# A MoE layer on one core: every chunk of an expert's weights as a high and a low part, one low part per expert on GpSimd

## The chip, the cores and the metric

The kernel runs on one NeuronCore of a Trainium2 chip. The metric is the device time of one execution in microseconds (us). The engines are named as the profile names them: PE (matrix multiplication; its weight loads are listed as PEld), DVE (vector engine), ACT (scalar engine), POOL (GpSimd) and SP (here it issues the loads of the weights). Each engine works through its own instructions strictly in order; semaphores tie the engines together.

## The reference

One layer of a decoder on 2048 tokens of width 1024: a mixer (input projection, retention heads, short convolution, output projection) and a hierarchical mixture of experts. Each token picks one of 8 groups, then 2 of that group's 8 experts, so that there are 64 experts. Everything is float32. The part that the change touches is the expert block:

```python
def run_block(args):
    tok, e = args
    xb = t_pad[tok]
    hb = jax.nn.silu(xb @ w_gate[e]) * (xb @ w_up[e])
    return hb @ w_down[e]
```

`w_gate` and `w_up` are 1024 x 512 per expert, `w_down` is 512 x 1024. The outputs of the experts are weighted, added to the residual stream, and normalised (final RMSNorm).

## The kernel before, in words

The program has two stages. The dense stage (mixer, router, lists of tokens) ends at about 940 us; then the experts run one after the other, 96 token slots each, to the end.

**One expert.** Its three matrices are cut into 24 chunks of 128 rows by 512 columns: 8 of w_gate (`w` = 0 in the code), 8 of w_up (1), and 8 of w_down (2), of which chunk `c` belongs to row block `c // 2` and column half `c % 2`. The weights arrive as units of four chunks (1 MB each, line 639, issued by SP into a set of buffers that are reused in turn).

**Split products.** A float32 product is made of three matmuls in the faster format float32r (lines 739 to 741, `mm3`): high part of the tokens times high part of the weight, high times low, low times high. The parts of a weight are made for a *piece*, which is two neighbouring chunks (128 x 1024): ACT copies the piece into float32r, which rounds it (line 679, `split_hi`), and DVE subtracts this from the original (line 685, `split_lo`). A piece has one of six places (four tiles `ring`, two tiles `part`), and its parts are made five pieces ahead (`LEAD`) of the matmuls that use it, so `split_hi` waits until PE has done with the piece that stood in that place.

**The plain chunks.** Chunks 6 and 7 of w_down (the last piece) are not split: `plain` picks them, and line 1056 multiplies them as plain float32 straight from the unit's buffer, with the third row block's tokens in `ewhole`. So an expert has 11 pieces, and DVE makes 11 low parts.

**The order of the work.** A stream written out by hand sets it: gate of expert q (8 chunks), up of q (8), then down of q-1 (8). What else an engine does is put in at places of this stream:

- PE transposes the hidden rows of q-1 after gate (line 758, `ph`), and the tokens of q+1 after up (line 730, `pxg`); ACT and DVE make their high and low parts (lines 764 and 765; 733 and 734: `xhi`, `xlo`). Before, 765 works on 128 x 288, and line 763 copies the remaining 96 columns whole.
- DVE multiplies gate and up (line 751, `hrow`), and adds the result of down to the token rows (line 778, twice per expert, from the PSUM tile `acc`).
- ACT takes the sum of squares of finished rows (line 784) and scales them (line 792).
- POOL, for each expert from the ninth on: fetches token rows by an indirect DMA (710), makes a row of weights (771), two tiny operations on the sums (785, 786), fetches residual rows (717, behind the transposes `pxg`), multiplies the rows scaled by ACT with the row of weights (795, 96 x 1024, two inputs in SBUF), and writes them out (822). For the first eight experts the rows are written without 771, 785, 786, 792 and 795.

Of the kernel before, what the change touches and what calls it, by code (L numbers as in the profile page):

```python
# [10 lines left out]
F32 = mybir.dt.float32  # L11
F32R = mybir.dt.float32r
# [3 lines left out]
AF = mybir.ActivationFunctionType  # L16
OP = mybir.AluOpType
AX = mybir.AxisListType

P = 128  # L20
# [5 lines left out]
KF = FF // P  # L26
# [5 lines left out]
CAP = 96  # L32
# [51 lines left out]
def hybrid_layer(ctx: ExitStack, tc: tile.TileContext, x, xT, norm1, w_in, gn_w, conv_w, w_o, norm2, norm2r,  # L84
                 r_w, r_b, w_gate, w_up, w_down, final_w, con, rot, empty, out):
    nc = tc.nc
    act, dve, pool, pe, sp = nc.scalar, nc.vector, nc.gpsimd, nc.tensor, nc.sync
# [47 lines left out]
    raws, parts = {}, {}  # L135
# [41 lines left out]
    hT, xraw = {}, {}  # L177
# [448 lines left out]
    EX = {}  # L626
# [18 lines left out]
    estream = []  # L645
# [15 lines left out]
            loaded.add(i)  # L661


    def plain(w, c):
        return w == 2 and c >= 6


    pieces = [(q, w, c) for q, w, c in estream if c % 2 == 0 and not plain(w, c)]
    ppos = {u: i for i, u in enumerate(pieces)}

    def split_hi(i):
# [10 lines left out]
    def split_lo(i):  # L682
        if i < len(pieces):
            hi, lo, src = parts[pieces[i]]
            dve.tensor_tensor(lo, src, hi.bitcast(F32), op=OP.subtract)  # L685

    rows_dma = {}

# [10 lines left out]
    def row_of(q):  # L699
        return row_all(q)[:CAP]  # L700
# [18 lines left out]
                                    bounds_check=S - 1, oob_is_err=False)  # L719
        moved("g", q, i)  # L720

    NH = 3

    def xpose(q):
        g, w = row_of(q), EX["work"]
        hi, lo = (w.tile([P, KD, CAP], F32R, name="x" + n) for n in ("hi", "lo"))
        for half in range(2):
            p = bank("pxg")
            for j in range(4):
                pe.transpose(p[:, j * P:j * P + CAP], g[:, half * 4 + j::KD], ident[:CAP, :CAP])  # L730
            pv = p.rearrange("p (k t) -> p k t", k=4)[:, :, :CAP]
            ks = slice(half * 4, half * 4 + 4)
            act.activation(hi[:, ks], pv, AF.Copy)
            dve.tensor_tensor(lo[:, ks], pv, hi[:, ks].bitcast(F32), op=OP.subtract)  # L734
        EX["xT", q] = hi, lo, None

    def mm3(o, ahi, alo, w, first, last):
        whi, wlo = w
        pe.matmul(o, ahi, whi, start=first, stop=False)  # L739
        pe.matmul(o, ahi, wlo, start=False, stop=False)  # L740
        pe.matmul(o, alo, whi, start=False, stop=last)  # L741
# [12 lines left out]
    def hpose(q):  # L754
        w = EX["work"]
        p = bank("ph")
        for k in range(KF):
            pe.transpose(p[:, k * P:k * P + CAP], EX["h", q][:, k::KF], ident[:CAP, :CAP])
        n = NH
        hi, lo = (w.tile([P, n, CAP], F32R, name="e" + v) for v in ("hi", "lo"))  # L760
        whole = w.tile([P, KF - n, CAP], F32, name="ewhole")
        pv = p.rearrange("p (k t) -> p k t", k=KF)[:, :, :CAP]
        act.activation(whole, pv[:, n:], AF.Copy)
        act.activation(hi, pv[:, :n], AF.Copy)
        dve.tensor_tensor(lo, pv[:, :n], hi.bitcast(F32), op=OP.subtract)
        EX["hT", q] = hi, lo, whole

    def weights(q, m=None):
        e = order[q]
# [58 lines left out]
    start = {}  # L828
# [131 lines left out]
    i = TB - 1  # L960
# [33 lines left out]
    w = ctx.enter_context(tc.tile_pool(name="work", bufs=1, side="right", reuse_waits="tile"))  # L994
# [28 lines left out]
    def later(q):  # L1023
        return q >= NG

    ps = {}
    for i, (q, wi, c) in enumerate(estream):
        if c % 4 == 0:
            done = upos[q, 2 * wi + c // 4] - 1
            if not AT <= done < AT + NFIRST:  # L1030
                load_unit(done + NRAW + (NFIRST if done < AT else 0))
        if (q, wi, c) in ppos:
            split_hi(ppos[q, wi, c] + LEAD)
            split_lo(ppos[q, wi, c] + LEAD)
        if i in (36, 40, 44):
            two = pair(FIRST[i // 4 - 9])
            if i < 44:
                EX["rows"] += two
                for j in (2, 1):
                    clear(len(EX["rows"]) - j)  # L1040
                    if i == 36:
                        gather(5 - j)
            else:
                EX["fw"], EX["fwm"] = (t[:CAP] for t in two)
                sp.dma_start(EX["fw"], bass.AP(tensor=final_w.tensor, offset=final_w.offset, ap=[[0, CAP], [1, D]]))
        n = q, 2 * wi + c // 4
        cs = slice(c % 4 * 512, c % 4 * 512 + 512)
        if plain(wi, c):
            wt = raws[n][:, cs]
        else:  # L1050
            wt = [t[:, c % 2 * 512:c % 2 * 512 + 512] for t in parts[q, wi, c - c % 2][:2]]

        def mm(o, stats, k, last):
            hi, lo, whole = stats
            if plain(wi, c):
                pe.matmul(o, whole[:, k - hi.shape[1]], wt, start=False, stop=last)  # L1056
            else:
                mm3(o, hi[:, k], lo[:, k], wt, k == 0, last)

        if wi < 2:  # L1060
            if c == 0:
                ps[wi] = acc.tile([P, 512], F32, name="acc")[:CAP]
            mm(ps[wi], EX["xT", q], c, c == 7)
            if wi == 0 and c == 0:
                if q > 1:
                    gather(q + 3)
                if later(q - 2):
                    weights(q - 2)
            if wi == 0 and c == 2 and 1 < q < NG + 2:
                put_rows(q - 2)  # L1070
            if wi == 0 and c == 4 and later(q - 2):
                norm1_rows(q - 2)
            if c == 7:
                if wi == 0:
                    gate_act(q, ps[0])
                    if q:
                        hpose(q - 1)
                else:
                    up_act(q, ps[1])
                    if q + 1 < NE:  # L1080
                        xpose(q + 1)
                        regather(q + 1)
        else:
            if c < 2:
                ps[2 + c] = acc.tile([P, 512], F32, name="acc")[:CAP]
            k, half = divmod(c, 2)
            mm(ps[2 + half], EX["hT", q], k, k == KF - 1)
            if q < NE - 1:
                if c == 4 and later(q - 1):
                    norm2_rows(q - 1)  # L1090
                    put_rows(q - 1)
                    if q == NE - 2:
                        weights(q)
                        weights(q + 1, EX["fw"])
                if c == 7:
                    add_rows(q, (ps[2], ps[3]))
                if c == 4 and q == NE - 2:
                    hpose(NE - 1)
            else:
                if c == 1:  # L1100
                    norm1_rows(q - 1)
                if c == 2:
                    r = row_of(q - 1)
                    dve.tensor_tensor(r, r, EX["m", q - 1], op=OP.mult)
                    act.activation(r, r, AF.Copy, scale=EX["ss", q - 1])
                    put_rows(q - 1)
                if c >= 6:
                    finish(q, half, ps[2 + half])
# [109 lines left out]
```

## Time and profile before

| | |
|---|---|
| median of 3 runs | 2124.74 us (2124.18 to 2127.75) |
| the profiled execution | 2125.29 us, its span 2123.5 us |
| busy over the span | PE 98%, DVE 80%, ACT 61%, POOL 38% |
| DMA | 578.81 MB, mean 273 GB/s |
| chain that ended last | lines 739 to 741 and 1056 on PE, then ACT, POOL and DVE for the last rows |

The profile lists each engine's instructions with a start and a length, and for a gap ahead of one the engine or transfer that ended it. The length of an instruction that follows another without a gap overlaps with its neighbour's a little, so what one costs is read from start to start. The length also holds the time in which an instruction stands blocked after its start. The shares are means over both stages; the expert stage is read by itself, below.

### The profile page before, as it was taken

What the parts mean: (1) busy time and instruction counts of PE and PEld (TensorE: products, weight loads), DVE (VectorE), ACT (ScalarE), POOL (GpSimd) and SP (SyncE); (2) the same over time, 40 slices, a digit from 0 to 9 for tenths busy, and PEclk for the clock granted to TensorE, in tenths of its full rate; (3) what the DMA queues carried; (4) which work ended last, traced back from release to release, by engine and by line L of the source; (5) the groups of instructions that cost most, each with busy time, mean ns of one, the idle gap of its engine ahead of it and who ended that gap; (6) DMA issues with size and microseconds to landing.
All of it is one profiled execution on the core that took longest, in us unless ns stands there. A gap on an engine that the chain in (4) does not pass through costs nothing. (4 is left out here: it accounts for less than half of the span.)

```text
span 2123.5 us, 28824 instructions
## 1 busy us (share of the span) xinstructions
PE 2087.7 (98%) x9801; PEld 1581.2 (74%) x9802; DVE 1704.2 (80%) x2460; ACT 1303.0 (61%) x1945; POOL 810.5 (38%) x871
## 2 busy tenths in 40 slices
PE   8999999999999999969999999999999999999998
PEld 7888888888888888856666666666666666666665
DVE  4657666775676467478889999999999999999997
ACT  4324433443334432458778888888888888888885
POOL 0010023001210022053334555466666666666657
PEclk9999999999999999979999999999999999999999
DMA  8345244534434354768999999999999999999991
GB/s 269 108 126 169 90 141 133 159 113 135 144 110 159 94 172 144 283 238 311 386 392 379 388 386 388 385 385 393 390 384 388 383 388 389 385 391 392 389 393 52
DMA packets 142279, 578.81 MB, mean 273 GB/s; under 512 B 29616, under 2 KB 29968, under 8 KB 92912
## 3 DMA queue, kind: packets, MB, share of 16 engines
q1 hardware_dynamic: 113456, 526.48, 66.1%
q0 software_dynamic: 28672, 50.46, 6.4%
q8 instruction: 77, 1.26, 0.2%
q14 instruction: 74, 0.61, 0.1%
HBM read 576.76 MB, written 52.59 MB: 296 GB/s over the span
## 5 line engine op out<-in xcount | busy, mean ns | idle before, releaser
L685 DVE TENSOR_TENSOR ring<-unit,ring 128x1024 fp32r<-128x1024 f32 x470 | 614.5, 1338 | 37.6 <-ACT ring L679 36.0
L679 ACT ACTIVATE ring<-unit 128x1024 fp32r<-128x1024 f32 x470 | 491.4, 1056 | 117.4 <-PE acc L741 111.5
L297 PE MATMUL acc<-hhi,ring 128*128 128x512 f32 x1280 | 404.5, 393 | 7.0 <-ACT ring L172 5.4
L685 DVE TENSOR_TENSOR part<-unit,part 128x1024 fp32r<-128x1024 f32 x234 | 309.5, 1343 | 18.2 <-ACT part L679 17.5
L173 DVE TENSOR_TENSOR ring<-wraw,ring 128x512 fp32r<-128x512 f32 x256 | 172.6, 687 | 185.3 <-ACT ring L172 185.3
L172 ACT ACTIVATE ring<-wraw 128x512 fp32r<-128x512 f32 x256 | 153.7, 625 | 264.3 <-issue 111.1
L739 PE MATMUL acc<-ring,xhi 128*96 128x512 f32 x688 | 291.8, 424 | 0.1
L297 PEld LDWEIGHTS acc<-hhi,ring 128*128 128x128 f32 x1280 | 241.4, 189 | 56.6 <-ACT ring L172 5.1
L679 ACT ACTIVATE part<-unit 128x1024 fp32r<-128x1024 f32 x234 | 245.7, 1057 | 56.8 <-PE acc L741 53.0
L741 PE MATMUL acc<-ring,xlo 128*96 128x512 f32 x688 | 271.0, 394 | 0.4 <-DVE xlo L734 0.4
L740 PE MATMUL acc<-ring,xhi 128*96 128x512 f32 x688 | 271.2, 394 | 0.0
L297 PE MATMUL acc<-hlo,ring 128*128 128x512 f32 x640 | 250.2, 391 | 0.0
L297 PE MATMUL acc<-ring,mix 128*128 128x512 f32 x768 | 183.8, 394 | 0.0
L297 PEld LDWEIGHTS acc<-ring,mix 128*128 128x128 f32 x768 | 141.8, 188 | 28.1
L297 PE MATMUL acc<-ring,hhi 128*128 128x512 f32 x512 | 162.2, 398 | 0.0
L739 PEld LDWEIGHTS acc<-ring,xhi 128*96 128x96 f32 x688 | 113.1, 164 | 53.6 <-issue 9.6
L740 PEld LDWEIGHTS acc<-ring,xhi 128*96 128x96 f32 x688 | 111.5, 162 | 53.3 <-issue 11.2
L741 PEld LDWEIGHTS acc<-ring,xlo 128*96 128x96 f32 x688 | 112.0, 163 | 49.7 <-DVE xlo L734 1.1
L739 PE MATMUL acc<-part,xhi 128*96 128x512 f32 x336 | 141.9, 422 | 0.0
L297 PEld LDWEIGHTS acc<-hlo,ring 128*128 128x128 f32 x640 | 120.9, 189 | 24.2
L741 PE MATMUL acc<-part,xlo 128*96 128x512 f32 x336 | 132.0, 393 | 0.0
L740 PE MATMUL acc<-part,xhi 128*96 128x512 f32 x336 | 132.0, 393 | 0.0
(230 smaller groups left out, 3744.4 us busy)
## 6 DMA issues: line engine op xcount, KB each, us to landing
unit<-in_w_down_dram SPq DMA_DIRECT2D x128, 1024.0 KB, 12.2
unit<-in_w_gate_dram SPq DMA_DIRECT2D x128, 1024.0 KB, 7.2
unit<-in_w_up_dram SPq DMA_DIRECT2D x128, 1024.0 KB, 9.7
wraw<-in_w_in_dram SPq DMA_DIRECT2D x225, 256.0 KB, 2.9
wraw<-in_w_o_dram SPq DMA_DIRECT2D x64, 256.0 KB, 2.9
xs<-in_x_dram SPq DMA_DIRECT2D x16, 512.0 KB, 4.7
x<-in_x_dram SPq DMA_DIRECT2D x16, 512.0 KB, 4.2
out_dram<-x SPq DMA_DIRECT2D x16, 512.0 KB, 3.9
```

The source lines that it names most:

```text
L172: act.activation(hi, src, AF.Copy)
L173: dve.tensor_tensor(lo, src, hi.bitcast(F32), op=OP.subtract)
L297: pe.matmul(o, l, r, start=first and j == 0, stop=last and j == 2)
L679: act.activation(t[:, 0], src, AF.Copy)
L685: dve.tensor_tensor(lo, src, hi.bitcast(F32), op=OP.subtract)
L739: pe.matmul(o, ahi, whi, start=first, stop=False)
L740: pe.matmul(o, ahi, wlo, start=False, stop=False)
L741: pe.matmul(o, alo, whi, start=False, stop=last)
```

## The change

All 24 chunks of an expert are split: `plain`, `NH`, `ewhole` and the matmul at line 1056 are gone, chunks 6 and 7 of w_down become the twelfth piece (2, 6) of an expert, and take the three float32r matmuls each. The parts of the hidden rows are made for all four row blocks (128 x 384 in one operation on ACT and one on DVE). The low part of piece (2, 6) is made by POOL, all others by DVE as before. The changed file is shorter, so in it line 685 is 682, 679 is 675, 792 is 784, 795 is 787, 771 is 763, 785 and 786 are 777 and 778, 765 is 757, 751 is 746, 734 is 729, 733 is 728, 784 is 776, 745 is 740, 717 is 714, 710 is 707, and DVE's 778 is 770.

```diff
--- before.py
+++ after.py
@@ -661,11 +661,7 @@
             loaded.add(i)
 
 
-    def plain(w, c):
-        return w == 2 and c >= 6
-
-
-    pieces = [(q, w, c) for q, w, c in estream if c % 2 == 0 and not plain(w, c)]
+    pieces = [(q, w, c) for q, w, c in estream if c % 2 == 0]
     ppos = {u: i for i, u in enumerate(pieces)}
 
     def split_hi(i):
@@ -682,7 +678,8 @@
     def split_lo(i):
         if i < len(pieces):
             hi, lo, src = parts[pieces[i]]
-            dve.tensor_tensor(lo, src, hi.bitcast(F32), op=OP.subtract)
+            eng = pool if pieces[i][1:] == (2, 6) else dve
+            eng.tensor_tensor(lo, src, hi.bitcast(F32), op=OP.subtract)
 
     rows_dma = {}
 
@@ -718,8 +715,6 @@
                                     in_offset=bass.IndirectOffsetOnAxis(ap=EX["ix"][:, e:e + 1], axis=0),
                                     bounds_check=S - 1, oob_is_err=False)
         moved("g", q, i)
-
-    NH = 3
 
     def xpose(q):
         g, w = row_of(q), EX["work"]
@@ -732,7 +727,7 @@
             ks = slice(half * 4, half * 4 + 4)
             act.activation(hi[:, ks], pv, AF.Copy)
             dve.tensor_tensor(lo[:, ks], pv, hi[:, ks].bitcast(F32), op=OP.subtract)
-        EX["xT", q] = hi, lo, None
+        EX["xT", q] = hi, lo
 
     def mm3(o, ahi, alo, w, first, last):
         whi, wlo = w
@@ -756,14 +751,11 @@
         p = bank("ph")
         for k in range(KF):
             pe.transpose(p[:, k * P:k * P + CAP], EX["h", q][:, k::KF], ident[:CAP, :CAP])
-        n = NH
-        hi, lo = (w.tile([P, n, CAP], F32R, name="e" + v) for v in ("hi", "lo"))
-        whole = w.tile([P, KF - n, CAP], F32, name="ewhole")
+        hi, lo = (w.tile([P, KF, CAP], F32R, name="e" + v) for v in ("hi", "lo"))
         pv = p.rearrange("p (k t) -> p k t", k=KF)[:, :, :CAP]
-        act.activation(whole, pv[:, n:], AF.Copy)
-        act.activation(hi, pv[:, :n], AF.Copy)
-        dve.tensor_tensor(lo, pv[:, :n], hi.bitcast(F32), op=OP.subtract)
-        EX["hT", q] = hi, lo, whole
+        act.activation(hi, pv, AF.Copy)
+        dve.tensor_tensor(lo, pv, hi.bitcast(F32), op=OP.subtract)
+        EX["hT", q] = hi, lo
 
     def weights(q, m=None):
         e = order[q]
@@ -1044,18 +1036,11 @@
                 EX["fw"], EX["fwm"] = (t[:CAP] for t in two)
                 sp.dma_start(EX["fw"], bass.AP(tensor=final_w.tensor, offset=final_w.offset, ap=[[0, CAP], [1, D]]))
         n = q, 2 * wi + c // 4
-        cs = slice(c % 4 * 512, c % 4 * 512 + 512)
-        if plain(wi, c):
-            wt = raws[n][:, cs]
-        else:
-            wt = [t[:, c % 2 * 512:c % 2 * 512 + 512] for t in parts[q, wi, c - c % 2][:2]]
+        wt = [t[:, c % 2 * 512:c % 2 * 512 + 512] for t in parts[q, wi, c - c % 2][:2]]
 
         def mm(o, stats, k, last):
-            hi, lo, whole = stats
-            if plain(wi, c):
-                pe.matmul(o, whole[:, k - hi.shape[1]], wt, start=False, stop=last)
-            else:
-                mm3(o, hi[:, k], lo[:, k], wt, k == 0, last)
+            hi, lo = stats
+            mm3(o, hi[:, k], lo[:, k], wt, k == 0, last)
 
         if wi < 2:
             if c == 0:
```

How this moves instructions, for an expert in the middle of the second stage. First POOL, from the fetch of token rows to the product with the row of weights, before:

```order
L710 DMA pair<-h_rows,ix 128x1024
L771 TENSOR_SCALAR pair<-pair,sec,nsec 96x1024
L785 TENSOR_TENSOR oss<-oss,eps 96x1
L786 TENSOR_TENSOR oss<-oss,expo 96x1
L703 MEMSET spacer 1x1
L717 DMA pair<-out_dram,ix 128x1024
L795 TENSOR_TENSOR row_7831<-row_7831,pair 96x1024
```

and of the change:

```order
L707 DMA pair<-h_rows,ix 128x1024
L763 TENSOR_SCALAR pair<-pair,sec,nsec 96x1024
L777 TENSOR_TENSOR oss<-oss,eps 96x1
L778 TENSOR_TENSOR oss<-oss,expo 96x1
L682 TENSOR_TENSOR ring<-unit,ring 128x1024
L700 MEMSET spacer 1x1
L714 DMA pair<-out_dram,ix 128x1024
L787 TENSOR_TENSOR row_7831<-row_7831,pair 96x1024
```

The subtraction of the piece stands between the tiny operations on the sums and the fetch of the residual rows; everything else keeps its order.

DVE, from the low part of the hidden rows (`elo`) to the addition of the result of down to the token rows, before:

```order
L765 TENSOR_TENSOR elo<-ph,ehi 128x288
L685 TENSOR_TENSOR ring<-unit,ring 128x1024 x3
L685 TENSOR_TENSOR part<-unit,part 128x1024
L751 SCALAR_TENSOR_TENSOR hrow<-acc,li,sg 96x512
L734 TENSOR_TENSOR xlo<-pxg,xhi 128x384 x2
L685 TENSOR_TENSOR part<-unit,part 128x1024
L685 TENSOR_TENSOR ring<-unit,ring 128x1024 x2
L778 TENSOR_TENSOR row_7831<-acc,row_7831 96x512 x2
```

and of the change:

```order
L757 TENSOR_TENSOR elo<-ph,ehi 128x384
L682 TENSOR_TENSOR part<-unit,part 128x1024
L682 TENSOR_TENSOR ring<-unit,ring 128x1024 x2
L746 SCALAR_TENSOR_TENSOR hrow<-acc,li,sg 96x512
L729 TENSOR_TENSOR xlo<-pxg,xhi 128x384 x2
L682 TENSOR_TENSOR ring<-unit,ring 128x1024
L682 TENSOR_TENSOR part<-unit,part 128x1024 x2
L682 TENSOR_TENSOR ring<-unit,ring 128x1024
L770 TENSOR_TENSOR row_7831<-acc,row_7831 96x512 x2
```

Between `elo` and `hrow` there are three subtractions of pieces on DVE and no longer four, and between `xlo` and the two additions four and no longer three; in all there are still eleven per expert.

ACT, from the high parts of the tokens (`xhi`) to the silu of gate (`sg`), before:

```order
L733 ACTIVATE xhi<-pxg 128x384 x2
L679 ACTIVATE part<-unit 128x1024 x2
L679 ACTIVATE ring<-unit 128x1024
L792 ACTIVATE row_7831<-row_7831,oss 96x1024
L679 ACTIVATE ring<-unit 128x1024 x3
L784 ACTIVATE ojunk_13070,oss<-row_7832 96x1024
L679 ACTIVATE part<-unit 128x1024
L745 ACTIVATE sg<-acc 96x512
```

and of the change:

```order
L728 ACTIVATE xhi<-pxg 128x384 x2
L675 ACTIVATE ring<-unit 128x1024
L675 ACTIVATE part<-unit 128x1024 x2
L784 ACTIVATE row_7831<-row_7831,oss 96x1024
L675 ACTIVATE ring<-unit 128x1024 x4
L776 ACTIVATE ojunk_13220,oss<-row_7832 96x1024
L675 ACTIVATE part<-unit 128x1024
L740 ACTIVATE sg<-acc 96x512
```

The scaling of the finished rows (`row_7831<-row_7831,oss`) still follows three splits behind `xhi`; behind it there are four splits up to the sum of squares (`ojunk`) and no longer three. The fourth subtraction on DVE ahead of the two additions therefore belongs to a split that stands behind the scaling, while before the last one ahead of them belonged to a split in front of it.

## Rows read from the trace of the kernel before

**Rows 1.** Busy time by stretch; columns as the header says

```profile
core 0: us, PE busy (x) PEld busy (x) DVE busy (x) ACT busy (x) POOL busy (x), PEclk, DMA share, GB/s
960.00:1143.00 183.00, 183.00 (x822) 127.02 (x821) 164.09 (x171) 138.11 (x168) 60.91 (x65) 1.00 0.93 363
1143.00:2086.00 943.00, 943.00 (x4238) 655.10 (x4237) 902.68 (x878) 773.68 (x984) 568.24 (x513) 1.00 0.97 383
```

**Rows 2.** Timeline of PE: start us, length us, engine, line, operation, out<-in, count

```profile
1502.15 1.88 PE L1056 MATMUL acc<-unit,ewhole 128*96 128x512 f32 x4
...
1504.10 0.39 PE L740 MATMUL acc<-ring,xhi 128*96 128x512 f32 x1
1504.33 0.40 PE L741 MATMUL acc<-ring,xlo 128*96 128x512 f32 x1
...
1509.41 0.61 PE L758 MATMUL ph<-cons,hrow 96*128 96x96 f32 x4
...
1527.69 0.61 PE L758 MATMUL ph<-cons,hrow 96*128 96x96 f32 x4
```

**Rows 3.** Timeline of DVE in the same expert; in brackets idle time before and releaser

```profile
1500.53 2.34 DVE L685 TENSOR_TENSOR part<-unit,part 128x1024 fp32r<-128x1024 f32 x2
1502.80 1.21 DVE L685 TENSOR_TENSOR ring<-unit,ring 128x1024 fp32r<-128x1024 f32 x1
1503.93 1.27 DVE L778 TENSOR_TENSOR row<-acc,row 96x512 f32<-96x512 f32 x2
1505.13 4.50 DVE L685 TENSOR_TENSOR ring<-unit,ring 128x1024 fp32r<-128x1024 f32 x3
1509.92 1.26 DVE L685 TENSOR_TENSOR part<-unit,part 128x1024 fp32r<-128x1024 f32 x1 [0.29 <-ACT part L679]
1511.11 0.45 DVE L765 TENSOR_TENSOR elo<-ph,ehi 128x288 fp32r<-128x288 f32 x1
1511.78 1.56 DVE L685 TENSOR_TENSOR part<-unit,part 128x1024 fp32r<-128x1024 f32 x1 [0.22 <-ACT part L679]
...
1516.66 0.74 DVE L751 SCALAR_TENSOR_TENSOR hrow<-acc,li,sg 96x512 f32<-96x512 f32 x1
1517.32 1.01 DVE L734 TENSOR_TENSOR xlo<-pxg,xhi 128x384 fp32r<-128x384 f32 x2
1518.25 1.21 DVE L685 TENSOR_TENSOR ring<-unit,ring 128x1024 fp32r<-128x1024 f32 x1
```

**Rows 4.** Timeline of POOL in the same expert

```profile
1503.15 3.13 POOL L795 TENSOR_TENSOR row<-row,pair 96x1024 f32<-96x1024 f32 x1 [3.13 <-ACT row L792]
...
1510.58 1.68 POOL L771 TENSOR_SCALAR pair<-pair,sec,nsec 96x1024 f32<-96x1024 f32 x1
...
1516.72 1.13 POOL L717 DMA_INDIRECT pair<-out_dram,ix  x1 [1.75 <-PE pxg L730]
```

**Rows 5.** POOL's line 795: shortest, median and longest ns, first and last start

```profile
...
L795 POOL TENSOR_TENSOR row<-row,pair x23: 2373/2572/3129, 1137.7 to 2051.3; 96x1024 f32<-96x1024 f32 x23
```

**Rows 6.** The same for POOL's line 771

```profile
L771 POOL TENSOR_SCALAR pair<-pair,sec,nsec x56: 1194/1310/3381, 1119.3 to 2109.0; 96x1024 f32<-96x1024 f32 x56
```

**Rows 7.** The same for POOL's line 487, before the experts

```profile
L487 POOL TENSOR_TENSOR wraw<-wraw,n2b x4: 2360/2384/2400, 895.4 to 923.7; 128x1024 f32<-128x1024 f32 x4
```

**Rows 8.** The same for DVE's line 522, before the experts

```profile
L522 DVE TENSOR_SCALAR pen<-cons,i x16: 230/231/2428, 285.0 to 924.5; 128x8 f32<-128x8 f32 x16
```

**Rows 9.** Timeline of DVE around one of these

```profile
896.41 1.47 DVE L522 TENSOR_SCALAR pen<-cons,i 128x8 f32<-128x8 f32 x1
```

**Rows 10.** Timeline of POOL at that place

```profile
895.45 2.40 POOL L487 TENSOR_TENSOR wraw<-wraw,n2b 128x1024 f32<-128x1024 f32 x1 [1.12 <-ACT wraw L486]
```

**Rows 11.** Timeline of ACT in the expert of Rows 3

```profile
1501.93 1.13 ACT L792 ACTIVATE row<-row,oss 96x1024 f32<-96x1024 f32 x1
...
1505.46 1.06 ACT L679 ACTIVATE ring<-unit 128x1024 fp32r<-128x1024 f32 x1 [1.45 <-PE acc L741]
```

**Rows 12.** Waits of SP's DMA queue: total us, times, longest

```profile
SPq L639 <- PE acc L1056: 392.4, 51, 8.1
```

## The prediction

> **What bounds the kernel now.** I read the busy time by stretch first. From 960 us on PE is busy for the whole of both stretches (183.00 of 183.00 us, 943.00 of 943.00) at a granted clock of 1.00; from 1143 us DVE is at 902.68 of 943 (95.7%), ACT at 82.0%, POOL at 60.3%, DMA at a share of 0.97 [rows 1]. A busy PE proves little, since matmuls are pipelined, so the timeline of PE comes next: the transposes of the hidden rows recur at 1509.41 and 1527.69, one expert is 18.27 us (18.28 by these two rows), and no gap ahead of a matmul is marked [rows 2]. PE sets the pace now, and DVE is the engine just behind it.
>
> Third are DVE and POOL side by side, because the change gives POOL a subtraction to do. A subtraction of 128 x 1024 costs 1.135 us of DVE from start to start (1500.53 to 1502.80 are two) and shows 1.21. But three of them from 1505.13 took 4.50 instead of 3.48, and the one at 1511.78 took 1.56 [rows 3]. In both cases POOL was at work: its product at line 795 ran to 1503.15 + 3.13 = 1506.28, and the first of the three can only have started then; line 771 ran to 1512.26 [rows 4]. The two additions at 1503.93, which read one operand from PSUM, ran beside line 795 at 0.60 each from start to start, unharmed. The clearest case lies ahead of the experts: DVE's line 522, on 8 columns, takes 231 ns in the median and up to 2428 [rows 8], and the instance of 1.47 us ended at 897.88 [rows 9], when POOL's line 487 ended, at 897.85 [rows 10]. So a DVE operation of this kind stands still until POOL's ends.
>
> The Trainium skill, page "SBUF — State Buffer", section "Who interferes with whom", states this as a rule: a DVE instruction with two SBUF inputs contends with a GpSimd instruction that reads SBUF, the port is held for the whole instruction, and a DVE instruction with one SBUF input goes free. The trace agrees, for the additions beside line 795 too. Applied blindly, with every large POOL operation charged in full, the rule would give the worst case among the rivals below.
>
> **The change, part by part** (per expert).
>
> *PE.* The four records of line 1056 are two plain chunks; from 1502.15 to 1504.10, less the one matmul of 0.23 (1504.10 to 1504.33) that lies between, they cost 1.72 [rows 2]. In their place come six matmuls of 0.23, 1.38. PE's need falls by 0.34, to 17.93.
>
> *ACT.* One more split, 1.06 [rows 11]; the two activations on the hidden rows become one over the same columns, which I count at nothing. 82.0% of 18.27 is 14.99, so 16.05 after. That stays under 17.93: not a bound.
>
> *DVE, its own work.* Eleven subtractions at 1.135 are 12.49; two additions 1.20 (1503.93 to 1505.13); `hrow` 0.66; two `xlo` 0.93, that is 0.465 each; the low part of the hidden rows now has the size of an `xlo`, 0.46, where it cost 0.37 or so [rows 3]. Sum 15.74, if nobody blocks it.
>
> *POOL.* The added subtraction has two SBUF inputs and 128 x 1024 elements, as line 487, which takes 2.38 undisturbed [rows 7]. POOL has 11.0 us of busy time in 18.27, so there is room for 2.4 more. Queued behind it are the fetch of the residual rows, which waits 1.75 for the transposes anyway [rows 4] and whose rows are added an expert later, and line 795, which idled 3.13 for ACT. The result is wanted by PE five pieces (6.9 us) after the split is issued: 1.06 for the split, up to 1.1 for the current DVE operation and 2.38 leave over 2 us. I charge POOL's queue nothing.
>
> *SP.* The buffer of the second half of w_down came free behind line 1056, for which the loads waited 392.4 us in 51 waits [rows 12]. Now POOL's subtraction frees it, which is due before PE gets there. The loads start no later; DMA needs 0.97 of 18.27, 17.7, per expert. No term.
>
> *What DVE loses to POOL.* POOL's large readers of SBUF are then three: line 795 with 2.37 at its shortest [rows 5], line 771 with 1.19 [rows 6], and the new 2.38, together 5.94. What falls beside additions, `hrow`, `xlo` and `elo` (3.25 of DVE's 15.74) costs nothing, the rest is lost.
> - The new one: between 0.79 (all of `hrow` and `xlo`, 1.59, beside it) and 2.38. I take 2.38: POOL starts when ACT has made the split, and in DVE's queue subtractions stand next there, ahead of `hrow`.
> - Line 795: about 1.0 now (4.50 − 3.48), because the additions come just as it starts. After the change the last subtraction ahead of the additions belongs to a split that ACT does behind the scaling of the rows, and line 795 starts when this scaling ends. So four subtractions, not the additions, are next on DVE. Between 1.0 and 2.37; I take 2.0, with most of one `xlo` beside it.
> - Line 771: it started 4.30 after the end of line 795 (1506.28 to 1510.58) [rows 4]; DVE does 3.8 subtractions in this time, finishes the fourth and comes to the additions, whose 1.20 cover it. Between 0 and 1.19; I take 0. The tiny operations between them: 0.
>
> Sum 15.74 + 2.38 + 2.0 = 20.1 us, against 17.93 for PE: DVE becomes the bound, and what PE gains is given away. An expert costs 1.85 more than 18.27.
>
> *How often.* Line 771 runs from 1119.3 to 2109.0 [rows 6], 54 periods of 18.27: 54 × 1.85 = 100 us. In the nine or so before, POOL has neither 771 nor 795; DVE needs at most 15.74 + 2.38 = 18.12 there, so 0.15 to 0.34 is gained: −2. From the profiled execution, 2125.3 (span 2123.5 and 1.8 around it; the median is 0.6 lower): 2125.3 + 100 − 2 = 2223 us.
>
> **Rivals.**
> 1. *POOL does not block, PE stays the bound: faster.* This needs the loss to stay under 17.93 − 15.74 = 2.19 per expert. For it: DVE loses little now (1.02 and 0.35 in the expert of rows 3), and the new operation might fall wholly beside PSUM work. Against it: 5.94 − 3.25 = 2.69 is lost even if every PSUM operation has POOL beside it and DVE never idles. It would give 2125.3 − 64 × 0.34 = 2103.5 us.
> 2. *Nearly full cover.* 15.74 + 2.69 = 18.43, or a loss of one us more: 54 × 0.16 = 9 to 54 × 0.8 = 43, so 2132 to 2166. For it: phases lock, and they did so well before. Against it: the orders of DVE and ACT around the scaling.
> 3. *No cover.* Line 771 or the new one always meets subtractions: 15.74 + 5.94 = 21.68, 54 × 3.41 = 184, so 2307 us. (That is what the rule of the Trainium skill's page "SBUF — State Buffer", above, gives when each operation is charged in full.) PE would stand still for 3.7 us of each expert; its clock, 1.00 in rows 1, could fall, which no row of an expert shows and I do not price.
> 4. *POOL delivers late*, so that the twelfth piece holds PE and not DVE's eleven. The two us of slack above speak against it; each us of lateness would be 63 us. I count it in 3.
>
> **How the numbers follow.** DVE-bound with 19.1 to 21.1 per expert: 0.80, which is 54 × 0.85 = 46 to 54 × 2.83 = 153, less 2: 2169 to 2276; the predicted time is its middle case. Rival 1: 0.06. Rival 2: 0.05, a part of it within 0.2% (4.2 us), which is about what a measurement of this kernel can tell from no change. Rivals 3 and 4: 0.09. Range 2170 to 2280. Faster 0.05, same 0.03 (a little from rivals 1 and 2 each), slower 0.92.
>
> **What would show it.** Right: DVE busy at 99% or more from about 1143 us; gaps ahead of PE's matmuls that DVE's subtraction ended; experts of about 20 us from the tenth on and of 18.0 before; POOL's subtraction at 2.4 to 3.5 with a DVE subtraction beside it that ends 1.1 after it; the mean subtraction at 1.21 + 4.4 / 11 = 1.6; line 795 beside subtractions and line 771 beside additions. Wrong: PE busy without gaps and experts of 17.9 (rival 1), or PE's gaps ended by POOL (rival 4).

## The result, and the profile after

The changed kernel takes 2259.19 us (median of 4, 2258.74 to 2261.57) against 2126.24 before: a ratio of 1.0626, 95% interval 1.0613 to 1.0639. The forecast was 2223 us, slower; its range, 2170 to 2280, holds the time.

Where the 133.5 us between the two spans (2257.0 and 2123.5) lie, read from the transposes of the hidden rows, once per expert: the first ten experts take 17.95 us each instead of 18.27 (−3), the next 52, the heavy experts below, take 20.66 (+124), the closing part takes 10 us more, and the dense stage ended 2.5 us later.

Busy time by stretch, the first ten experts and then the 52; they are to be held against [rows 1]:

```profile
core 0: us, PE busy (x) PEld busy (x) DVE busy (x) ACT busy (x) POOL busy (x), PEclk, DMA share, GB/s
964.00:1143.00 179.00, 179.00 (x839) 129.22 (x838) 175.36 (x166) 146.24 (x166) 159.24 (x75) 1.00 0.95 373
1143.00:2217.00 1074.00, 982.26 (x4368) 673.07 (x4367) 1062.17 (x886) 812.47 (x987) 1019.36 (x566) 0.98 0.88 336
```

PE is no longer busy throughout the heavy experts, and DVE is busy for 1062 of 1074 us (98.9%). On the timeline of PE, the first and the last row here are 52 experts apart (1074.39 / 52 = 20.66). The two rows between them end gaps of the two kinds that [rows 2] did not have; the brackets tell what ended them:

```profile
1143.16 0.60 PE L753 MATMUL ph<-cons,hrow 96*128 96x96 f32 x4
...
1511.17 0.48 PE L735 MATMUL acc<-ring,ehi 128*96 128x512 f32 x1 [1.82 <-POOL spacer L700]
...
1598.04 0.74 PE L735 MATMUL acc<-ring,xhi 128*96 128x512 f32 x1 [1.99 <-DVE ring L682]
...
2217.55 0.60 PE L753 MATMUL ph<-cons,hrow 96*128 96x96 f32 x4
```

DVE in one expert, to be held against [rows 3]:

```profile
1601.32 1.27 DVE L770 TENSOR_TENSOR pair<-acc,pair 96x512 f32<-96x512 f32 x2
1602.52 4.32 DVE L682 TENSOR_TENSOR ring<-unit,ring 128x1024 fp32r<-128x1024 f32 x3
1606.77 1.21 DVE L682 TENSOR_TENSOR part<-unit,part 128x1024 fp32r<-128x1024 f32 x1
1607.90 0.54 DVE L757 TENSOR_TENSOR elo<-ph,ehi 128x384 fp32r<-128x384 f32 x1
1608.37 1.21 DVE L682 TENSOR_TENSOR part<-unit,part 128x1024 fp32r<-128x1024 f32 x1
1609.50 2.35 DVE L682 TENSOR_TENSOR ring<-unit,ring 128x1024 fp32r<-128x1024 f32 x2
1611.77 0.74 DVE L746 SCALAR_TENSOR_TENSOR hrow<-acc,li,sg 96x512 f32<-96x512 f32 x1
1612.43 1.00 DVE L729 TENSOR_TENSOR xlo<-pxg,xhi 128x384 fp32r<-128x384 f32 x2
1613.36 2.42 DVE L682 TENSOR_TENSOR ring<-unit,ring 128x1024 fp32r<-128x1024 f32 x1
1615.70 4.61 DVE L682 TENSOR_TENSOR part<-unit,part 128x1024 fp32r<-128x1024 f32 x2
```

and POOL beside it, against [rows 4]:

```profile
1601.20 3.44 POOL L763 TENSOR_SCALAR pair<-pair,sec,nsec 96x1024 f32<-96x1024 f32 x1
1604.62 6.14 POOL L777 TENSOR_TENSOR oss<-oss,eps 96x1 f32<-96x1 f32 x1
1610.84 1.45 POOL L778 TENSOR_TENSOR oss<-oss,expo 96x1 f32<-96x1 f32 x1
1612.28 2.42 POOL L682 TENSOR_TENSOR ring<-unit,ring 128x1024 fp32r<-128x1024 f32 x1
...
1616.81 2.40 POOL L787 TENSOR_TENSOR pair<-pair 96x1024 f32<-96x1024 f32 x1
```

DVE has not one gap here, but three subtractions are long. Of the three from 1602.52 the second stands until line 763 (the row of weights) ends at 1604.64, and together they take 4.32 instead of 3.48; the one at 1613.36 shows 2.42 while POOL's new subtraction runs to 1614.69; the pair from 1615.70 takes 4.61 instead of 2.35 beside line 787 (the product). The groups of subtractions over all heavy experts (count, busy us, mean ns); one takes 1.21 us when undisturbed:

```profile
L682 DVE TENSOR_TENSOR ring<-unit,ring 128x1024 fp32r<-128x1024 f32 x365 | 603.3, 1684 | 8.8 <-ACT ring L675 8.8
L682 DVE TENSOR_TENSOR part<-unit,part 128x1024 fp32r<-128x1024 f32 x208 | 316.7, 1542 | 1.5 <-ACT part L675 1.5
```

The mean over both rows is 1.63, so DVE loses 11 × 0.42 = 4.6 us per expert; 15.74 of own work and 4.6 are 20.4 of the 20.66.

The timeline of POOL shows something else too. Line 777 works on 96 single numbers and takes 6.14 us. Its shortest, median and longest (ns) in this kernel:

```profile
L777 POOL TENSOR_TENSOR oss<-oss,eps x55: 183/1153/6157, 1132.0 to 2245.5; 96x1 f32<-96x1 f32 x55
```

While it stood from 1604.62, DVE ran subtraction upon subtraction, with only `elo` between them. I read this as the exclusion in the other direction: POOL waits for DVE. Its own subtraction, queued behind, is then late. The gap of PE that ended at 1511.17 above did so when POOL's subtraction ended, at 1511.12:

```profile
1508.76 2.36 POOL L682 TENSOR_TENSOR ring<-unit,ring 128x1024 fp32r<-128x1024 f32 x1
```

The idle time of PE in the 52 experts, by what ended it (total us, times, longest; "spacer" is the next POOL line, whose semaphore carries the end of the subtraction):

```profile
...
PE acc L735 <- DVE ring L682: 48.5, 27, 2.0
PE acc L735 <- POOL spacer L700: 34.8, 39, 5.9
...
```

39 gaps, 34.8 us, are POOL's; 27, 48.5 us, DVE's. The longer gaps cost a little clock. PE stood for 1.99 us up to 1598.04, and in the 4 us from 1597 the granted clock was 0.58 (third column from the right), so mostly the lower of its two levels, 1.2 GHz. PE worked again from 1598.04, and in the 37 us from 1601, with PE busy for 35.53 of them, it was 1.00, the upper level, 2.4 GHz:

```profile
1597.00:1601.00 4.00, 2.96 (x7) 2.08 (x8) 4.00 (x4) 0.47 (x1) 3.60 (x3) 0.58 0.69 178
1601.00:1638.00 37.00, 35.53 (x162) 24.26 (x160) 37.00 (x32) 30.73 (x38) 35.88 (x19) 1.00 0.94 361
```

### The profile page after: what moved, and what is told of

Same layout as the page of the kernel before. It is cut to its first block, busy times and chain, and to the rows that moved or that the text cites. A ratio compares the mean times of both kernels' runs of the same rounds, so it can differ in the third digit from the quotient of the medians.

```text
span 2257.0 us, 29092 instructions
## 1 busy us (share of the span) xinstructions
PE 2119.6 (94%) x9929; PEld 1599.1 (71%) x9930; DVE 1875.8 (83%) x2460; ACT 1349.2 (60%) x1945; POOL 1366.6 (61%) x935
## 5 line engine op out<-in xcount | busy, mean ns | idle before, releaser
L682 DVE TENSOR_TENSOR ring<-unit,ring 128x1024 fp32r<-128x1024 f32 x449 | 729.3, 1654 | 12.9 <-ACT ring L675 12.4
L675 ACT ACTIVATE ring<-unit 128x1024 fp32r<-128x1024 f32 x512 | 528.8, 1055 | 152.8 <-PE acc L736 146.8
L682 DVE TENSOR_TENSOR part<-unit,part 128x1024 fp32r<-128x1024 f32 x255 | 376.9, 1496 | 2.0 <-ACT part L675 2.0
L735 PE MATMUL acc<-ring,xhi 128*96 128x512 f32 x768 | 311.3, 405 | 50.2 <-DVE ring L682 48.7
L736 PE MATMUL acc<-ring,xlo 128*96 128x512 f32 x768 | 306.4, 399 | 8.0 <-DVE xlo L729 8.0
L734 PE MATMUL acc<-ring,xhi 128*96 128x512 f32 x768 | 310.1, 404 | 0.1
L675 ACT ACTIVATE part<-unit 128x1024 fp32r<-128x1024 f32 x256 | 267.5, 1054 | 14.6 <-PE acc L736 12.4
L735 PEld LDWEIGHTS acc<-ring,xhi 128*96 128x96 f32 x768 | 125.6, 164 | 125.2 <-DVE ring L682 80.1
L763 POOL TENSOR_SCALAR pair<-pair,sec,nsec 96x1024 f32<-96x1024 f32 x56 | 197.4, 3526 | 2.9
L777 POOL TENSOR_TENSOR oss<-oss,eps 96x1 f32<-96x1 f32 x55 | 182.3, 3315 | 1.5 <-ACT ojunk L776 1.5
L682 POOL TENSOR_TENSOR ring<-unit,ring 128x1024 fp32r<-128x1024 f32 x63 | 163.0, 2588 | 17.0 <-ACT ring L675 17.0
L734 PEld LDWEIGHTS acc<-ring,xhi 128*96 128x96 f32 x768 | 127.6, 166 | 48.8 <-ACT xhi L728 0.5
```

The source lines that it names most:

```text
L675: act.activation(t[:, 0], src, AF.Copy)
L682: eng.tensor_tensor(lo, src, hi.bitcast(F32), op=OP.subtract)
L763: pool.tensor_scalar(m, EX["fw"], EX["sec"][:, e:e + 1], EX["nsec"][:, e:e + 1], op0=OP.mult, op1=OP.add)
L777: pool.tensor_tensor(ss, ss, eps[:CAP], op=OP.add)
```

## The experiments

**All low parts on DVE.** One part of the change undone.

```diff
-            eng = pool if pieces[i][1:] == (2, 6) else dve
-            eng.tensor_tensor(lo, src, hi.bitcast(F32), op=OP.subtract)
+            dve.tensor_tensor(lo, src, hi.bitcast(F32), op=OP.subtract)
```

> The changed kernel with the twelfth low part on DVE as well; nothing else differs. Theory (DVE sets the pace, and POOL's subtraction blocks it for about 2.0 us per expert): DVE takes 1.14 us of own work and loses 2.0 us of blocking, so an expert falls from 20.6 to about 19.8 us in the 53 heavy periods, about 2215 us; the first ten experts stay at 17.95 (own work 16.9); no wait of PE ends with POOL. Rival (what costs is the twelfth piece and the new order around the scaling of the rows, not POOL's subtraction): no relief, and DVE, the busiest engine, gets 1.14 us more per expert: 2259 + 60 = about 2320 us.

Measured: 2281.01 us, ratio 1.073 (1.0712 to 1.0748), so 1% slower than the changed kernel. Neither number came. DVE idles for 13% of the 1074 us here (busy for 931.98), so its own work and its blocked time do not fill an expert either. POOL and then DVE in one expert:

```profile
1678.23 8.38 POOL L762 TENSOR_SCALAR pair<-pair,sec,nsec 96x1024 f32<-96x1024 f32 x1
1686.58 4.16 POOL L776 TENSOR_TENSOR oss<-oss,eps 96x1 f32<-96x1 f32 x1
```

```profile
1679.48 1.21 DVE L681 TENSOR_TENSOR part<-unit,part 128x1024 fp32r<-128x1024 f32 x1
1680.61 0.54 DVE L756 TENSOR_TENSOR elo<-ph,ehi 128x384 fp32r<-128x384 f32 x1
1681.08 1.21 DVE L681 TENSOR_TENSOR part<-unit,part 128x1024 fp32r<-128x1024 f32 x1
1682.21 3.48 DVE L681 TENSOR_TENSOR ring<-unit,ring 128x1024 fp32r<-128x1024 f32 x3
1685.62 0.74 DVE L745 SCALAR_TENSOR_TENSOR hrow<-acc,li,sg 96x512 f32<-96x512 f32 x1
1686.28 1.01 DVE L728 TENSOR_TENSOR xlo<-pxg,xhi 128x384 fp32r<-128x384 f32 x2
```

The row of weights, 1.19 at its shortest [rows 6], took 8.38. DVE ran subtractions without a gap meanwhile, with one operation (`elo`) between them that has an operand in PSUM, where PE writes its results. If POOL's own work is the last 1.19 us, it came in at 1686.61 − 1.19 = 1685.4 (an estimate), at the end of the run, when `hrow` and the two `xlo` were next. The first tiny operation then waited for the next run. ACT's scaling (line 783 here) needs the result of the second, and ACT works in order, so the splits behind the scaling were late, and DVE waited for them (total us, times, longest):

```profile
DVE ring L681 <- ACT ring L675: 142.0, 50, 2.9
ACT pair L783 <- POOL oss L777: 130.5, 28, 4.9
...
ACT row L783 <- POOL oss L777: 102.0, 22, 4.9
```

By this reading the twelfth subtraction on DVE costs time because it makes DVE's runs longer, and POOL gets nowhere during them.

**The scaling behind the split.**

```diff
-                if c == 4 and later(q - 1):
+                if c == 6 and later(q - 1):
                     norm2_rows(q - 1)
```

> The changed kernel with the scaling of the finished rows on ACT and the product with the row of weights on POOL put behind the split at chunk 6 of w_down, so that the split of the last subtraction ahead of the two additions is again in front of the scaling, as before the change. Theory (the product costs DVE 1.9 us per expert because subtractions and not the additions are beside it): its block falls towards 0.9 us, 1.0 us less in each of 53 periods, about 2206 us. Rival (DVE is late by its own queue, so that the product meets subtractions wherever ACT stands, or what is won there is lost at the row of weights, which has the additions beside it now): 2250 to 2260 us.

Measured: 2287.46 us, ratio 1.0759 (1.0741 to 1.0777). A miss for both: the experts became uneven, most at about 18 and the others at 23 to 29, where PE waited for POOL's subtraction (20 gaps, up to 7.0 us):

```profile
PE acc L735 <- POOL spacer L700: 100.8, 20, 7.0
```

The new place of ACT's scaling and of the product on POOL behind it moved the time to another wait. This run can't be used to size the block of line 787.

**The kernel before, with one low part made a second time, by POOL.**

```diff
             dve.tensor_tensor(lo, src, hi.bitcast(F32), op=OP.subtract)
+            if pieces[i][1:] == (2, 4):
+                pool.tensor_tensor(lo, src, hi.bitcast(F32), op=OP.subtract)
```

> The kernel before, with 11 pieces and its plain chunks, where POOL makes the low part of piece (2, 4) once more, behind DVE and over the same values: only a POOL subtraction is added, nothing on DVE, ACT or PE. Theory (the port): DVE's need in the heavy periods is 15.65 own, 1.65 blocked now and 2.0 to 2.4 more, 19.3 to 19.7 us against 18.27, so 53 x 1.0 to 1.4 us more, 2180 to 2200 us; the first ten experts stay at 18.27 (15.65 + 2.4 is below it). Rival (a POOL subtraction runs beside DVE for free, the cost is in the 24 split chunks): 2125 us.

Measured: 2321.36 us (2309.64 to 2339.86), ratio 1.0916 (1.0842 to 1.099). The rival falls: a POOL subtraction costs in the old kernel too, with its 11 pieces and plain chunks. The size is beyond both. PE needs what POOL writes here, and the trace shows that it stood for POOL; from 1143 to 2217 us the granted clock was 0.93, so in part its lower level, where the kernel before had 1.00 up to 2086:

```profile
PE acc L742 <- POOL spacer L705: 145.0, 26, 6.2
```

**The tiny operations behind POOL's subtraction.**

```diff
...
+    def norm1_pool(q):
+        e, ss = order[q], EX["ss", q]
         pool.tensor_tensor(ss, ss, eps[:CAP], op=OP.add)
         pool.tensor_tensor(ss, ss, EX["expo"][:, e:e + 1], op=OP.pow)
...
+            if wi == 1 and c == 4 and later(q - 2):
+                norm1_pool(q - 2)
...
```

> The changed kernel with POOL's two tiny operations on the sums of squares behind its subtraction instead of in front of it. In the changed kernel PE waited 39 times, 41 us in all, for POOL's subtraction, since the row of weights and these two waited up to 6 us for DVE ahead of it. Theory (DVE's sum of own work and blocked time sets the pace, the place of PE's wait does not): the waits for POOL go, PE waits for DVE's subtractions instead, 2245 to 2262 us. Rival (POOL's lateness is a cost of its own): 41 us less, about 2218 us.

Inconclusive: one of its four executions took 2266.65 us and three took 2334.87 to 2336.53, and only one of the longer ones, 2334.87, has a trace. In that one experts of 17.95 and 26.4 us take turns, and PE stood for POOL's subtraction for 152.5 us (23 gaps between 1200 and 2200 us). No execution came into the theory's range, and 41 us less, as the rival had it, was seen in none either.

**POOL fills instead of subtracting.**

```diff
+            if pieces[i][1:] == (2, 6):
+                pool.memset(lo.bitcast(F32), 0.0)
+            else:
+                dve.tensor_tensor(lo, src, hi.bitcast(F32), op=OP.subtract)
```

> The changed kernel, where POOL fills the low part of piece (2, 6) with zeros instead of subtracting (this leaves out the low part of that piece): POOL's operation stands in the same place, PE waits for it as before, but it reads nothing from SBUF. Theory (a POOL operation that reads SBUF and a DVE subtraction exclude each other, in both directions): DVE has 15.74 us of own work and loses 1.0 to 1.9 to the product and up to 0.8 to the row of weights, 16.7 to 18.4 us per expert, so PE sets the pace at 17.95 in most experts, 2103 to 2130 us. Rival (the twelve pieces, the order around the scaling and the place in POOL's queue cost the time, whatever POOL's operation reads): above 2230 us.

Measured: 2196.31 us, ratio 1.0329 (1.0312 to 1.0346): 63 us better than the changed kernel, in which the same place of the queue holds a reader of 2.4 us and not a fill of 0.95. Three experts of four take 17.95, the fourth 24.6. The groups of POOL (busy us, mean ns):

```profile
L765 POOL TENSOR_SCALAR pair<-pair,sec,nsec 96x1024 f32<-96x1024 f32 x49 | 284.4, 5804 | 2.4
...
L682 POOL MEMSET ring<- 128x1024 f32 x48 | 45.4, 945 | 0.0
```

The fill takes 0.95, and no subtraction of DVE was longer beside it. What is left are the readers in front of it: the row of weights takes 5.8 in the mean instead of 1.19. In every fourth expert the fill comes so late behind them that PE stands for it (12 gaps, 44.5 us); after the gap of 3.72 us that ended at 1581.66 the granted clock was 0.52 for the 7 us from 1581, so nearly all of them at the lower level, 1.2 GHz, and the expert is 6.7 us longer, more than the gap. The theory was right on the operation, and its range ended 66 us too low, since the remaining readers wait.

**No large POOL operation.** All low parts on DVE, and:

```diff
-        pool.tensor_scalar(m, EX["fw"], EX["sec"][:, e:e + 1], EX["nsec"][:, e:e + 1], op0=OP.mult, op1=OP.add)
+        act.activation(m, EX["fw"], AF.Identity, scale=EX["sec"][:, e:e + 1], bias=EX["nsec"][:, e:e + 1])
...
-        if q < NE - 4:
-            act.activation(r, r, AF.Copy, scale=ss)
-        else:
-            pool.tensor_scalar(r, r, ss, None, op0=OP.mult)
-        pool.tensor_tensor(r, r, m, op=OP.mult)
+        dve.scalar_tensor_tensor(r, r, ss, m, op0=OP.mult, op1=OP.mult)
```

> 24 split chunks with all twelve low parts on DVE, the product of the rows with their scale and the row of weights as one operation on DVE, and the row of weights made by ACT; POOL keeps its DMAs and the two tiny operations. Theory (port): DVE's own work is 15.74 + 1.14 + 1.14 = 18.0 us, nothing large blocks it, 18.0 to 18.2 us per expert, 2105 to 2120 us, faster than both. Rival (the two tiny operations, which read SBUF, wait for DVE's run of subtractions to end, 4.2 us for the first of them with all low parts on DVE, and the scaling waits for them): 20 us and more, above 2230 us.

Measured: 2130.29 us, ratio 1.0017 (1.0008 to 1.0027): level with the kernel before, and 129 us (5.7%) better than the changed one, though DVE now does two operations of this length more per expert. Its groups:

```profile
L681 DVE TENSOR_TENSOR ring<-unit,ring 128x1024 fp32r<-128x1024 f32 x412 | 483.4, 1212 | 0.0
L681 DVE TENSOR_TENSOR part<-unit,part 128x1024 fp32r<-128x1024 f32 x206 | 245.6, 1211 | 0.0
```

The mean is the undisturbed 1.21, and no subtraction took more than 1.23. With twelve of them the own work is 18.07, the experts take 17.95 (first ten) and 18.26 (the next 52). The rival falls, though the first tiny operation took up to 8.20 here. The theory holds but for the last 0.5%: the time is 10 us above its range, since from the twenty-second expert on every third takes 18.9. DVE's product waited for the second tiny operation 16 times, 11.6 us in all, which is about that much.

**A POOL subtraction that nobody waits for,** in the kernel before:

```diff
+            if pieces[i][1:] == (2, 4):
+                if "spare" not in EX:
+                    EX["spare"] = EX["work"].tile([P, 1024], BF16, name="spare")
+                pool.tensor_tensor(EX["spare"], src, hi.bitcast(F32), op=OP.subtract)
```

> The kernel before with one more POOL subtraction per expert, of the same operands as DVE's for piece (2, 4), into a tile that nobody reads (in bfloat16): PE doesn't wait for it. When PE did wait for a second POOL subtraction, the kernel took 2321 us, of which PE stood about 140 us waiting for POOL. Theory A (the price is the blocking of DVE): 15.65 + 1.65 + 2.0 to 2.4 is 19.3 to 19.7 us per expert in the heavy periods, 2180 to 2200 us. Theory B (the price is that POOL's operation itself waits for DVE, and what waits for POOL is late): 2125 to 2140 us. Neither, above 2250: POOL's queue as a whole is late, and with it the sums that the scaling on ACT waits for.

Measured: 2275.32 us, ratio 1.0701 (1.0683 to 1.0718). The time is 75 us above theory A's range and lies where the third outcome was put, but the reason given for that one is not in the trace: ACT's scaling waited for POOL's sums once, for 4.7 us. In kind it is theory A: DVE is busy for 939.98 of 943 us, and its mean subtraction (the groups below) is 1.69, 0.48 over the undisturbed 1.21, so 11 × 0.48 = 5.3 us are lost per expert where I had 3.7 to 4.1: 15.65 + 5.3 = 20.95, measured 20.9. Theory B falls: next to nothing waited for this operation (ACT, once, 1.8 us), and it costs 148 us.

```profile
L685 DVE TENSOR_TENSOR ring<-unit,ring 128x1024 fp32r<-128x1024 f32 x329 | 545.9, 1700 | 3.0 <-ACT ring L679 3.0
L685 DVE TENSOR_TENSOR part<-unit,part 128x1024 fp32r<-128x1024 f32 x166 | 273.5, 1675 | 0.0
```

**All low parts on DVE, the row of weights on ACT.** The first part of the diff of "No large POOL operation", without the second.

> 24 split chunks, all twelve low parts on DVE, and the row of weights made by ACT instead of POOL; the product stays on POOL. With the row of weights on POOL this kernel took 2281 us with DVE idle for 13% of the stage: the row of weights took 8.4 us instead of 1.2 and the first tiny operation 4.2, since they waited for DVE, and ACT waited 220 us for them in front of the scaling. Theory (POOL waits for DVE, and the scaling for POOL): with the row of weights gone from in front of them the sums come about 7 us earlier, the scaling waits no longer, and DVE's 16.9 own and 1.0 to 2.0 blocked set the pace, 18.0 to 18.9 us, 2110 to 2165 us. Rival (DVE's blocks and not POOL's lateness held that kernel): 1.2 us less per expert at most, 2215 to 2280 us.

Measured: 2248.5 us, ratio 1.0575 (1.0558 to 1.0593), 32 us less than with the row of weights on POOL, in the rival's range. The wait moved: the tiny operations pass now (0.27 in the median for the first), and the product waits. POOL, then DVE:

```profile
1646.12 6.00 POOL L786 TENSOR_TENSOR pair<-pair 96x1024 f32<-96x1024 f32 x1 [5.36 <-ACT pair L783]
```

```profile
1645.85 2.35 DVE L681 TENSOR_TENSOR part<-unit,part 128x1024 fp32r<-128x1024 f32 x2
1648.12 1.22 DVE L681 TENSOR_TENSOR ring<-unit,ring 128x1024 fp32r<-128x1024 f32 x1
1649.26 1.28 DVE L769 TENSOR_TENSOR pair<-acc,pair 96x512 f32<-96x512 f32 x2
1650.46 2.73 DVE L681 TENSOR_TENSOR ring<-unit,ring 128x1024 fp32r<-128x1024 f32 x1
```

It asks at 1646.12, the running subtraction and two more pass, and it runs beside the two additions: 6.00 instead of 2.37. The subtraction at 1650.46 then stands until it ends. The edit also made a wait of its own: ACT's row of weights (line 762) overwrites the tile that the product reads, so ACT stood until the product had ended, and the splits behind it were late for DVE:

```profile
ACT pair L762 <- POOL spacer L699: 185.3, 44, 4.2
```

So this run does not tell how much of the 2281 us was POOL's lateness ahead of the scaling.

**POOL's subtraction as the only large reader.** Product and scale on DVE and the row of weights on ACT, as above; the low part of piece (2, 6) stays on POOL.

> The changed kernel with POOL's subtraction kept, but the product of the rows with their scale and weights on DVE and the row of weights on ACT: the subtraction is then the only large operation with which POOL reads SBUF. Theory (a POOL subtraction costs DVE nearly its whole 2.38 us, as the first ten experts of the changed kernel show with 2.19): DVE has 15.74 + 1.20 own work and 2.2 to 2.4 blocked, 19.1 to 19.3 us per heavy expert against 17.95 for PE, 2175 to 2190 us. Rival (alone it finds gaps, or waits itself until DVE has some, and only several such operations together cost): 18.0 to 18.4 us, 2105 to 2130 us, level with the kernel that has no large POOL operation (2130 us).

Measured: 2214.91 us, ratio 1.0413 (1.0397 to 1.0429); the rival falls, and the theory holds in kind, 25 us above its range. An expert takes 19.87 against 18.26 with that low part on DVE, in two kernels that differ in this alone: POOL's doing it costs 1.6 us more than DVE's doing it. POOL and DVE:

```profile
1646.00 0.58 POOL L778 TENSOR_TENSOR oss<-oss,expo 96x1 f32<-96x1 f32 x1
1646.56 2.39 POOL L682 TENSOR_TENSOR ring<-unit,ring 128x1024 fp32r<-128x1024 f32 x1
```

```profile
1646.10 3.94 DVE L682 TENSOR_TENSOR ring<-unit,ring 128x1024 fp32r<-128x1024 f32 x1 [0.23 <-ACT ring L675]
```

POOL's tiny operation and the subtraction follow each other without a gap, and DVE's subtraction stands through both: 3.94, a loss of 2.73. That is more than the 2.2 to 2.4 of the expectation. Over the heavy experts the loss is 2.7 per expert.

**Half a last piece.** From "No large POOL operation": chunk 6 of w_down split, chunk 7 plain again.

```diff
+            n = 512 if (w, c) == (2, 6) else 1024
...
+        plain = (wi, c) == (2, 7)
...
+            if plain:
+                pe.matmul(o, EX["whole", q], wt, start=False, stop=last)
+                return
```

> The kernel without large POOL operations (24 split chunks, all low parts, scale and product on DVE, row of weights on ACT: 2130 us, DVE's own work 18.07 us per expert), with chunk 7 of w_down left plain, so that the last piece is half as wide. Theory (with POOL away, the larger of PE and DVE sets the pace): PE 17.95 + 0.86 - 0.69 = 18.12 us, DVE 18.07 - 0.53 = 17.54 us, so 18.12 against 18.27 before, 63 x 0.15 = 9 us less than before, 2112 to 2120 us. Rival (POOL's tiny operations and DMAs, late behind DVE, cost what the 18.9 us experts of that kernel showed): 2125 to 2135 us.

Measured: 2118.48 us (5 runs, 2118.37 to 2120.57), ratio 0.9964 (0.995 to 0.9977): 0.4% below the kernel before, and in the theory's range. Every expert takes 18.12 or 18.13. PE is busy throughout again, DVE for 920.55 of 943 us (columns as in the stretches above):

```profile
1143.00:2086.00 943.00, 943.00 (x4319) 667.89 (x4318) 920.55 (x989) 821.45 (x1043) 543.85 (x411) 1.00 0.96 384
```

## Why the prediction was right

*PE.* Six float32r matmuls for two plain chunks: 17.93 forecast, 17.95 in the first ten experts. Right; the last experiment, which splits one of the two plain chunks, turns a part of this gain into time.

*DVE becomes the bound.* Right: 98.9% busy, 27 of PE's gaps ended by its subtractions, and with the large POOL readers gone the extra time is gone ("No large POOL operation"). The mechanism, a POOL reader standing in front of DVE's subtraction, is shown by two pairs of runs that differ in it: a subtraction that nobody waits for, added or not (2275 and 2126), and the low part on POOL or on DVE with nothing else large (2215 and 2130). A fill against a subtraction (2196 and 2259) fits, but there the operation is also shorter.

*The sizes.* The forecast had 2.38 + 2.0 + 0 for the new subtraction, the product and the row of weights. Adding up, over the heavy experts, what each subtraction showed beyond 1.21, by the POOL operation that ended while it stood: 1.94 (with the tiny operation that runs right ahead of it), 1.92 and 0.79, 4.65 per expert in all. The mis-sized term is the row of weights, taken as covered by the two additions. In the expert shown it began as they did (1601.20), but ended only beside the second subtraction behind them, and cost 0.84. That the sum of the three came out only 0.27 too low is in part luck: the new subtraction cost 0.44 less than its term. With the idle time of DVE, 0.2, this makes 20.6 of 20.66.

*POOL's queue, charged nothing.* This is the step that failed. I gave POOL's subtraction two us of slack, with at most one DVE operation to wait for. The subtraction itself kept to that (2.39 in the median, 4.78 at most), but what stands in front of it in POOL's queue waited for several: 3.43 in the median for line 763, up to 6.16 for a tiny operation. So rival 4, POOL late, did occur beside the forecast: 39 gaps of PE, 34.8 us. How much of this adds to the time and how much only replaces a wait for DVE is not settled by a run; the one that should have told it was inconclusive. But DVE, which did the same own work, idled for only 11.8 of the 1074 us, so over its own and its blocked time it left room for no more than that, 0.2 us per expert.

*The rest of the miss* (36 us): 0.54 per heavy expert, 28 us, as above; the closing part, for which I had nothing, 10 us more, and the later end of the dense stage 2.5; against these, 52 heavy periods and not 54, 4 us less, and one us more won in the first ten.

*A sum that is off.* In rival 2, a loss of one us more would be 54 × 1.16 = 63 us, not 54 × 0.8 = 43. The forecast and its range do not use it.

*What I would have had wrong.* By the forecast's terms, all low parts on DVE take 15.74 + 1.14 + 2.0 = 18.9 us per expert, less than the changed kernel. They took 21.18 (2281 us). DVE's own and blocked time bounds the changed kernel, but one step beside it, as I read that run's waits, the bound is a ring: POOL waits for DVE's run, the scaling on ACT for POOL, the splits for the scaling, DVE for the splits.

The Trainium skill, page "SBUF — State Buffer", section "Who interferes with whom", says that whoever issues first holds the port for its whole instruction. For one operation against one the trace agrees: POOL's subtraction began at 1612.28, DVE's at 1613.36, and DVE's stood until POOL's ended at 1614.69. Where operations follow each other without a gap it does not, in either direction: the row of weights that began at 1678.23 ended behind five subtractions that began after 1679, and POOL's subtraction of 1646.56 went ahead of DVE's, which stood since 1646.10. The prediction also gave the same section's rule for a DVE operation with one SBUF input without its exception, the modes of DVE that use two ports. Line 522, which has one such tensor beside a number per partition, did stand for POOL [rows 9] [rows 10]; in which mode it ran, no run shows.

## What to carry to other kernels

Before work goes to GpSimd, look at what DVE runs beside it: where DVE's operations read two operands from SBUF, a GpSimd operation that reads SBUF can cost DVE its whole length, here 2.73 us (with part of a tiny operation right ahead of it) for work that DVE does in 1.14. Look in both directions: if DVE runs such operations without a gap, even a tiny GpSimd operation can take microseconds, up to 6.16 in the changed kernel, and whatever waits for it, through ACT and back to DVE, is late. When two engines exclude each other, moving one operation can shift the wait rather than remove it; here the time came back to that of the kernel before only when all large GpSimd readers were gone.

## What the runs showed of the hardware that was not expected

- POOL's operation on 96 x 1 took between 0.18 and 6.16 us in the changed kernel, and the row of weights (96 x 1024) between 1.2 and 8.41 over all runs. The long ones that were looked at stood while DVE ran subtractions without a gap. When exactly POOL gets in is open. The product came in beside two additions in one run (from 1649.26), the row of weights not beside two in another (from 1601.32). That one waited for one subtraction more, the one in the run with all low parts on DVE for five and more.
- A POOL fill of 128 x 1024 took 0.94 to 0.96 in every instance, whether or not DVE ran subtractions beside it.
- Two POOL readers without a gap between them kept DVE out through both (3.94).
- Within one execution of the changed kernel the heavy experts fall into different rhythms: mostly 19.5 and 21.65 in turn, in places 17.95 and 23 to 27.
